# A two-layer encoder trunk: x of the first MLP through DRAM, and the last 16 adaLN vectors made in halves during that MLP's first product

## The chip, the cores and the metric

The kernel runs on one core of a Trainium2 chip. The metric is the device time of one execution in microseconds (us); lower is better. Below, PE is TensorE (matmuls), DVE is VectorE, ACT is ScalarE, POOL is GpSimd and SP is SyncE, whose queue issues nearly all DMAs here.

## The reference, cut to what matters

The input is one sequence of 1024 positions with 1024 channels, and one conditioning vector c. There are two layers. Each has a mixer and a channel MLP, and both are normed, shifted, scaled and gated by vectors that come from c:

```python
cond = silu(c)
for i in range(2):
    mod = cond @ ada_w[i] + ada_b[i]             # 6 vectors of 1024 for each layer
    sh1, sc1, g1, sh2, sc2, g2 = split(mod, 6)
    h = rmsnorm(x, norm1_g[i]) * (1 + sc1) + sh1
    y = gqa_attention(h) if i == 0 else chunked_gmlp(h)
    x = x + g1 * y
    h = rmsnorm(x, norm2_g[i]) * (1 + sc2) + sh2
    x = x + g2 * (square(relu(h @ w_in[i])) @ w_out[i])
```

The vectors sh1 to g2 are called j = 0 to 5 in the kernel. Each is kept as 8 columns of 128 values (k = 0 to 7), so "an adaLN vector" (layer, j, k) is here one column of 128 numbers: 128 dot products of length 1024.

## The kernel before, in words

Everything is held transposed: a tile has 128 channels on the partitions and 512 positions (one half, `hf`) along the free axis. x is 16 such tiles, `x[hf][m]`. They sit in the 16 slots of the tag "x" (`xslot()`), which attention used for its keys before, and which the gMLP uses for other things after writing x out.

Every product runs in fp32 by splitting each operand into a high and a low part and doing three matmuls (L415 to L417 in a first product, L1073 to L1075 in a second one). The splits are the steady work of ACT (high part, L287, L400, L1057) and DVE (low part, L288, L401, L1058). Large products use a seven-multiplication scheme on 2x2 blocks (q = "1" to "7"), with sums of weights and sums of activations made on DVE and POOL.

The stages in order of time are: attention; its output product (`wo_mm`, L792 to L796), which adds to x; the first MLP (`mlp(0, ...)`) with a first product (`winograd`, 112 units of 12 matmuls) and a second product (`Out`, 112 units); the gMLP with its v product, u product and `Out` product (84 units); and the second MLP, again two products.

In an MLP the first product's hook `at(i)` is called after unit i. At i = HB = 2 it starts the norm of the right half of x (`norm_ss`, `norm_rb`), and from then on `forms_b` reads `x[1]` through the next eight units. The left half was read earlier by `forms_a`. Then x rests until the second product adds to it (`Out.add`, L1089, `x = out * gate + x`). When a tile of x is finished, `done` squares it on ACT (L231) and adds the square up on POOL or DVE (L235) for the next norm.

The adaLN vectors are made in three ways. Some are made by `Slabs` on POOL during attention. Most are made by `mod_load`: a 512 KB DMA of 128 rows of the weight (L141), one DVE instruction over 128x1024 that multiplies by the broadcast silu(c) and sums along the row (L145), the read of its accumulator, and a small add of the bias (L148). 32 of the list `pending` are done this way by the end of the output product of attention. The last 16 (layer 1, j = 3 and 5) are left for later: 12 of them in the second product of the first MLP, at units 14, 17, ... 47 (`MO`), and 4 in the `Out` product of the gMLP at units 16, 20, 24, 28 (`MG`). For each of the two stages the broadcast c is loaded again (`load_cond`, L134) and passed through Silu on ACT (`silu_cond`, L137). Their buffers come from the pool "c", which `cut(4)` opens at unit 8.

The gMLP already sends x through DRAM: `spill(hf)` stores x to `xd` (L1279), the slots are used by the v and u products, and `load_xs` reads x back (L1525) around the start of its `Out` product.

The order of instructions on an engine's queue is made by a planner from operands, buffers and modelled times; an instruction wrapped in `pin(...)` stays behind all that was written before it on its engine. The `mod_load` DVE instruction and the Silu are pinned; DMAs of `spill` and `load_xs` are not. Once made, the order is fixed, and each engine works it off in order, waiting wherever an operand is late.

Of the kernel before, what the change touches and what calls it, by code (L numbers as in the profile page):

```python
# [11 lines left out]
F32 = mybir.dt.float32  # L12
F32R = mybir.dt.float32r
AF = mybir.ActivationFunctionType
ALU = mybir.AluOpType
# [3 lines left out]
P = 128  # L19
D = 1024  # L20
KT = 8
# [15 lines left out]
def encoder_kernel(ctx: ExitStack, tc: tile.TileContext, t: dict, out: bass.AP):  # L37
    nc = tc.nc
    V, S, G, T = nc.vector, nc.scalar, nc.gpsimd, nc.tensor

    const = ctx.enter_context(tc.tile_pool(name="const", bufs=1))
    small = ctx.enter_context(tc.tile_pool(name="small", bufs=3))
# [4 lines left out]
    def nm(s):  # L47
        uid[0] += 1
        return f"{s}_{uid[0]}"

    def pin(ins):
        tc.keep_in_program_order(ins)

    def slot(dt=F32, shape=(P, 512)):
        return mem.tile(list(shape), dt, tag="t", name=nm("t"), bufs=SLOTS["t"])

    def xslot(dt=F32):
        return mem.tile([P, 512], dt, tag="x", name=nm("x"), bufs=SLOTS["x"])


    part = {}

    def cut(n):
        if part:
            part["es"].close()
        es = ExitStack()
        part.update(es=es, n=n, pool=es.enter_context(tc.tile_pool(name=nm("part"), bufs=1)))

    def cwide(dt=F32, shape=(1024,)):
        return part["pool"].tile([P] + list(shape), dt, tag="c", name=nm("c"), bufs=4)  # L70
# [54 lines left out]
    mod = const.tile([P, 2, 6, KT], F32, name="mod")  # L125
    adab = const.tile([P, 2, 6, KT], F32, name="adab")
# [1 line left out]
    ng = const.tile([P, 2, 2, KT], F32, name="ng")  # L128
    amod = const.tile([P, 2, 2, KT], F32, name="amod")
    cond = []  # L130

    def load_cond(tile_):
        cond[:] = [tile_]
        nc.sync.dma_start(tile_, t["cond"].broadcast_to([P, D]))  # L134

    def silu_cond():
        pin(S.activation(cond[0], cond[0], AF.Silu))  # L137

    def mod_load(layer, j, k, tag="w", late=True):
        raw = wide(tag)  # L140
        ld = nc.sync.dma_start(raw, t["ada"][layer, j * KT + k])  # L141
        if tag == "w" and late:
            pin(ld)
        acc = mod[:, layer, j, k : k + 1]
        ins = V.scalar_tensor_tensor(raw, raw, 1.0, cond[0], ALU.mult, ALU.mult, accum_out=acc)  # L145
        if late:
            pin(ins)
        V.tensor_tensor(acc, acc, adab[:, layer, j, k : k + 1], ALU.add)  # L148

    def mod_scale(layer, which, k):  # L150
        V.scalar_tensor_tensor(amod[:, layer, which, k : k + 1], mod[:, layer, 3 * which + 1, k : k + 1],
                               1.0, ng[:, layer, which, k : k + 1], ALU.add, ALU.mult)

    pending = [(0, j, k) for j in (2, 4, 3, 5) for k in range(KT)]
# [48 lines left out]
    def mods(n, tag="w"):  # L203
        for _ in range(min(n, len(pending))):
            layer, j, k = pending.pop(0)
            mod_load(layer, j, k, tag)
            if j in (1, 4):
                mod_scale(layer, j // 3, k)
# [31 lines left out]
    def norm_ss(sqs, bank):  # L240
        acc = sqs.acc
        ps = bank("ss")[:, :4]
        for j in range(4):
            T.matmul(ps[:, j : j + 1], acc[:, j * P : (j + 1) * P], ones[:, 0:1], start=True, stop=True)
        ms = small.tile([P, 4], F32, tag="ms", name=nm("ms"))
        V.tensor_scalar(ms, ps, 1.0 / D, EPS, ALU.mult, ALU.add)
        r = rsqrt_small(ms, 4)
        dg = slot()
        for j in range(4):
            V.tensor_scalar_mul(dg[:, j * P : (j + 1) * P], ident, r[:, j : j + 1])  # L250
        return dg
# [59 lines left out]
    def more(f, n=1, left=0):  # L311

        while f["todo"] and (n > 0 or (left is not None and len(f["todo"]) > left)):
            f["todo"].pop(0)()
            n -= 1
# [433 lines left out]
    x = [[None] * KT, [None] * KT]  # L749
# [52 lines left out]
    with ExitStack() as es:  # L802
# [117 lines left out]
        for i in range(nu + 2):  # L920
# [7 lines left out]
            for op in ORDER.split():  # L928
                f, w, j = op[0], int(op[1]), int(op[2])
# [31 lines left out]
    dram = ctx.enter_context(tc.tile_pool(name="dram", bufs=1, space=bass.MemoryType.DRAM))  # L961
# [175 lines left out]
    def spread(tiles, dst, spare, eng):  # L1137

        b11, b12, b21, b22 = (tiles[a] for a in ((0, 0), (0, 1), (1, 0), (1, 1)))
        t3 = spare()  # L1140
        eng.tensor_tensor(t3, b22, b12, ALU.subtract)
        eng.tensor_tensor(b12, b12, b11, ALU.subtract)
        eng.tensor_tensor(b11, b22, b12, ALU.subtract)
        eng.tensor_tensor(b21, b21, b11, ALU.subtract)
        return [lambda: nc.sync.dma_start(dst["7"], t3), lambda: nc.sync.dma_start(dst["5"], b12),
                lambda: nc.sync.dma_start(dst["6"], b11), lambda: nc.sync.dma_start(dst["4"], b21)]

    def early(q):
        return {(0, 0): "1", (1, 0): "2", (1, 1): "3"}.get(q)

    def forms_dram(n):
        return [{q: dram.tile([P, 512], F32, name=nm("hf")) for q in OUT_FORMS} for _ in range(n)]

    def mlp(layer, f, sqB, done, hook):
        hidden = forms_dram(16)
        out_ = Out(t["wm"][layer], hidden, 4, mod[:, layer, 5])
        cut(8)
        quad = {}
        stores = []

        def sink(c, m, hf):
            S.activation(c, c, AF.Relu)
            S.activation(c, c, AF.Square)
            p = m // 2
            quad[(m, hf)] = c
            q = early((m % 2, hf))
            if q:
                nc.scalar.dma_start(hidden[p][q], c)
                if q == "1" and p < FIRST:
                    del quad[(m, hf)]  # L1170
                elif q == "2" and p < FIRST:
                    quad[(m - 1, 0)] = slot()
                    nc.sync.dma_start(quad[(m - 1, 0)], hidden[p]["1"])
            else:
                tiles = {(j, h): quad.pop((m + j, h)) for j in range(2) for h in range(2)}
                stores.extend(spread(tiles, hidden[p], slot, V))

        n = 16 * 7
        rest = []

        def at(i):
            more(f, RW, None)
            if i == HB:
                rest.append(norm_ss(sqB, bank_y))
            elif i == HB + 1:
                rest[:] = forms_b(f, x[1], layer, 1, norm_rb(rest[0], bank_y), "5473")
            elif i > HB and rest:
                rest.pop(0)()
            if stores and i % 7 > 0 and i % 7 != 6:
                stores.pop(0)()  # L1190
            out_.ahead(i - n)

        winograd(lambda m: t["wi"][layer, m], 16, f, sink, FIRST, at)
        while stores:
            stores.pop(0)()

        def at_out(i):
            if i == MO[0] - 6:
                cut(4)
                if pending:  # L1200
                    load_cond(cwide())
            elif pending and i == MO[0] - 2:
                silu_cond()
            if len(pending) > 4 and i >= MO[0] and (i - MO[0]) % MO[1] < MO[2]:
                mods(1, "c")
            if hook and i >= out_.n - out_.tail:
                hook(i - out_.n + out_.tail)

        out_.run(at_out, done)

    wo_sums(1)
# [34 lines left out]
    def norm_hook(layer, which, bank):  # L1246
# [11 lines left out]
        return hook  # L1258

    mlp(0, fA, sqB, add_sq, norm_hook(1, 0, bank_y))  # L1260


    pieces = {}
    for ct in range(24):
        i, r = divmod(ct, 3)
# [4 lines left out]
        else:  # L1270
            pieces[ct] = ((2 * i + 1, 0, P),)

    xd = [[dram.tile([P, 512], F32, name=nm("xd")) for _ in range(KT)] for _ in range(2)]
    vd = [[dram.tile([2, P, 2, 256], F32, name=nm("vd")) for _ in range(4)] for _ in range(6)]
    st = small.tile([P, 8, 6, 6], F32, tag="st", name="st", bufs=1)

    def spill(hf):
        for k in range(KT):
            nc.sync.dma_start(xd[hf][k], x[hf][k])  # L1279

    def wino_v(f, hook):

# [128 lines left out]
    def gmlp(f, sqB, done, hook):  # L1411
# [78 lines left out]
        for p in range(12):  # L1490
            i = 7 * p
# [27 lines left out]
        upto(n + 9)  # L1519
        while stores:  # L1520
            stores.pop(0)()
        def load_xs(hf, odd):
            for k in range(odd, KT, 2):
                x[hf][k] = xslot()
                nc.sync.dma_start(x[hf][k], xd[hf][k])  # L1525

        load_xs(0, 0)
        XL = {2: (0, 1), 6: (1, 0), 10: (1, 1)}

        def at_out(i):  # L1530
            if i == MG[0] - 6:
                cut(4)
                load_cond(cwide())
            elif pending and i == MG[0] - 2:
                silu_cond()
            if pending and i >= MG[0] and (i - MG[0]) % MG[1] < MG[2]:
                mods(1, "c")
            if i in XL:
                load_xs(*XL[i])
            if i >= out_.n - out_.tail:  # L1540
                hook(i - out_.n + out_.tail)
# [23 lines left out]
FA = 3  # L1565
LO = 3
TG = ((0, 0), (1, 0), (1, 1), (0, 1))
MO = (14, 3, 1)
MG = (16, 4, 1)
LW = 5  # L1570
IG = 30
SW = 3
# [4 lines left out]
HB = 2  # L1577
# [80 lines left out]
```

## Time and profile before

| | |
|---|---|
| median of 3 runs | 2747.19 us (2745.71 to 2747.94) |
| the profiled execution's own time | 2744.76 us |
| its span | 2742.9 us |
| first product of the first MLP | starts at 679.0 us |
| second product of the first MLP | starts at 1004.7 us |
| v product of the gMLP | starts at 1333.7 us |
| `Out` product of the gMLP | starts at 1857.3 us |
| first product of the second MLP | starts at 2109.9 us |
| second product of the second MLP | starts at 2426.3 us |

A table of windows gives, for a stretch "from:to" of the span, the stretch's length and then the busy time and the number of instructions (x) of PE, PEld (weight loads), DVE, ACT and POOL, then the granted TensorE clock, the DMA engines' busy share and the GB/s moved. A row of a source line gives the count, then minimum/median/maximum duration in ns, then when the first and the last one started, then the shapes. A row of waits reads: who waited, for whom, us in total, how many times, the longest. A row of the timeline has the start, the time taken, the instruction, and in brackets the idle time of the engine before it and what ended it.

### The profile page before, as it was taken

How to read it: one execution, taken by the hardware profiler on the slowest of the kernel's cores; microseconds unless marked ns; L12 is line 12 of the kernel's file. 1: busy time of each engine (PE TensorE's matmuls, PEld its weight loads, DVE VectorE, ACT ScalarE, POOL GpSimd, SP SyncE). 2: the span in 40 equal slices, each digit the busy share in tenths (PEclk: the TensorE clock that was granted, in tenths of full speed). 3: DMA queues.
4: the chain of work that ended last, by engine and by line, in shares of the span. 5: the costliest groups of instructions: out<-in, count | busy, mean ns of one | idle time of the engine just before them, and what ended most of it. 6: DMA issues, size and time to landing. Idle time of an engine off the chain costs nothing. (4 is left out here: it accounts for less than half of the span.)

```text
span 2742.9 us, 37309 instructions
## 1 busy us (share of the span) xinstructions
PE 2642.3 (96%) x12804; PEld 2184.9 (80%) x12804; DVE 2275.4 (83%) x3191; ACT 1454.5 (53%) x2598; POOL 1063.8 (39%) x716
## 2 busy tenths in 40 slices
PE   7889999999899999999999999999989999999999
PEld 5668999887688887777778888887868688878877
DVE  7889888888887778998797777787998887789993
ACT  4448999964644455435443355444436554554442
POOL 2448777534300024451543255556541400034520
PEclk9999999999999999999999999999999999999999
DMA  7241111225164458826244345558642364478462
GB/s 263 71 138 47 62 55 55 80 95 182 66 210 151 160 205 313 293 81 206 79 134 131 108 166 180 181 189 315 234 131 66 111 205 149 162 260 287 142 203 70
DMA packets 200544, 427.52 MB, mean 156 GB/s; under 512 B 23137, under 2 KB 35425, under 8 KB 200354
## 3 DMA queue, kind: packets, MB, share of 16 engines
q1 hardware_dynamic: 173474, 387.37, 41.6%
q10 hardware_dynamic: 26880, 37.76, 3.7%
q8 instruction: 101, 1.65, 0.2%
q14 instruction: 89, 0.73, 0.1%
HBM read 306.56 MB, written 118.49 MB: 155 GB/s over the span
## 5 line engine op out<-in xcount | busy, mean ns | idle before, releaser
L1074 PE MATMUL out<-t,s 128*128 128x512 f32 x1232 | 487.0, 396 | 14.3 <-DVE t L288 14.3
L1073 PE MATMUL out<-t,s 128*128 128x512 f32 x1232 | 487.0, 396 | 6.8 <-ACT t L287 6.8
L1075 PE MATMUL out<-t,s 128*128 128x512 f32 x1232 | 485.8, 395 | 6.0 <-DVE s L1058 5.7
L415 PE MATMUL w<-t,s 128*128 128x512 f32 x1168 | 460.1, 395 | 0.5 <-ACT t L287 0.5
L416 PE MATMUL w<-t,s 128*128 128x512 f32 x1168 | 455.5, 391 | 1.5 <-DVE t L288 1.1
L417 PE MATMUL w<-t,s 128*128 128x512 f32 x1168 | 454.9, 389 | 0.9 <-DVE s L401 0.9
L288 DVE TENSOR_TENSOR t<-t,t 128x512 fp32r<-128x512 f32 x408 | 377.9, 940 | 28.7 <-ACT t L287 21.2
L287 ACT CAST t<-t 128x512 fp32r<-128x512 f32 x408 | 244.3, 617 | 157.9 <-DMA t<-hf 65.2
L400 ACT CAST s<-w 128x512 fp32r<-128x512 f32 x292 | 174.3, 619 | 229.7 <-PE w L417 164.1
L1074 PEld LDWEIGHTS out<-t,s 128*128 128x128 f32 x1232 | 234.9, 191 | 70.7 <-DVE t L288 21.3
L1073 PEld LDWEIGHTS out<-t,s 128*128 128x128 f32 x1232 | 234.4, 190 | 60.1 <-ACT t L287 11.0
L1075 PEld LDWEIGHTS out<-t,s 128*128 128x128 f32 x1232 | 234.8, 191 | 59.3 <-DVE s L1058 11.1
L401 DVE TENSOR_TENSOR s<-w,s 128x512 fp32r<-128x512 f32 x292 | 227.9, 789 | 59.0 <-ACT s L400 55.4
L1044 POOL TENSOR_TENSOR w<-w,t 128x512 f32<-128x512 f32 x32 | 53.0, 1658 | 557.2 <-DMA t<-in_wm_dram 279.3
L416 PEld LDWEIGHTS w<-t,s 128*128 128x128 f32 x1168 | 219.4, 188 | 51.0 <-DVE t L288 6.7
L415 PEld LDWEIGHTS w<-t,s 128*128 128x128 f32 x1168 | 219.2, 188 | 49.6 <-issue 3.4
L417 PEld LDWEIGHTS w<-t,s 128*128 128x128 f32 x1168 | 219.3, 188 | 46.4 <-DVE s L401 1.3
L1058 DVE TENSOR_TENSOR s<-t,s 128x512 fp32r<-128x512 f32 x240 | 212.2, 886 | 49.2 <-ACT s L1057 46.4
L1057 ACT CAST s<-t 128x512 fp32r<-128x512 f32 x240 | 147.6, 620 | 188.7 <-PE out L1075 115.6
L860 DVE TENSOR_TENSOR t<-t,t 128x512 fp32r<-128x512 f32 x256 | 164.3, 683 | 20.9 <-ACT t L854 20.9
L837 DVE TENSOR_REDUCE mx<-s 128x1 f32<-128x1024 f32 x128 | 156.6, 1224 | 23.7 <-PE s L834 22.4
L870 PE MATMUL o<-t,t 128*128 128x256 f32 x1024 | 163.7, 293 | 0.0
(247 smaller groups left out, 5438.1 us busy)
## 6 DMA issues: line engine op xcount, KB each, us to landing
t<-hf SPq DMA_DIRECT2D x320, 256.0 KB, 4.5
hf<-c SPq DMA_DIRECT2D x156, 256.0 KB, 2.1
w<-in_wi_dram SPq DMA_DIRECT2D x64, 512.0 KB, 4.3
hf<-c ACTq DMA_DIRECT2D x96, 256.0 KB, 2.0
c<-in_ada_dram SPq DMA_DIRECT2D x36, 512.0 KB, 4.7
w<-in_adan_dram SPq DMA_DIRECT2D x32, 512.0 KB, 3.3
t<-in_wm_dram SPq DMA_DIRECT2D x64, 256.0 KB, 5.3
wf<-w SPq DMA_DIRECT2D x64, 256.0 KB, 3.3
```

What stands on the lines that cost most here:

```text
L287: S.copy(hi, src)
L288: (eng or V).tensor_tensor(lo, src, f32(hi), ALU.subtract)
L400: S.copy(hi, src)
L401: V.tensor_tensor(lo, src, f32(hi), ALU.subtract)
L415: T.matmul(ps, hi[:, a], th, start=kt == 0, stop=False)
L416: T.matmul(ps, hi[:, a], tl, start=False, stop=False)
L417: T.matmul(ps, lo[:, a], th, start=False, stop=kt == 3)
L860: pin(V.tensor_tensor(lo, pt, f32(hi), ALU.subtract))
L1058: V.tensor_tensor(lo, src, f32(hi), ALU.subtract)
L1073: T.matmul(ps, hi[:, a], th, start=begin and kt == 0, stop=False)
L1074: T.matmul(ps, hi[:, a], tl, start=False, stop=False)
L1075: T.matmul(ps, lo[:, a], th, start=False, stop=end and kt == 3)
```

## The change

`spill`, `load_xs` and the DRAM tiles `xd` move ahead of `mlp`, and the first MLP uses them too: at unit HB + 10 = 12 of its first product all of x is stored to DRAM, and x is read back around the start of its second product, in the same four groups as in the gMLP (before unit 0, and after units 2, 6 and 10). In between, the 16 x slots are free for the new class `Halves`. It loads c as two broadcast tiles of 128x512 and passes each through Silu. It then makes each of the 16 vectors that are left from two loads of 128x512 and two DVE instructions of that size, whose sums go to a small tile; after the eight vectors of one j, one small add joins the halves and one adds the bias, for all eight at once. As written, steps are taken at units 20, 25, ... 95 (MX = 5), two vectors are loaded ahead at unit 12, and one more at each step. None of the new instructions is pinned.

The second product of the first MLP and the `Out` product of the gMLP lose their loads of c, their Silu and their 12 and 4 vectors; only `cut(4)` stays at unit 8 (`CUT`).

```diff
-    def load_cond(tile_): ...
-    def silu_cond(): ...
+    xd = [[dram.tile([P, 512], F32, name=nm("xd")) for _ in range(KT)] for _ in range(2)]
+    def spill(hf):
+        for k in range(KT):
+            nc.sync.dma_start(xd[hf][k], x[hf][k])
+    def load_xs(hf, odd):
+        for k in range(odd, KT, 2):
+            x[hf][k] = xslot()
+            nc.sync.dma_start(x[hf][k], xd[hf][k])
+    XL = {-1: (0, 0), 2: (0, 1), 6: (1, 0), 10: (1, 1)}
+    class Halves:
+        def __init__(self, todo):
+            self.todo, self.raw, self.part = list(todo), [], {}
+        def start(self):
+            self.cond = [xslot(), xslot()]
+            for h in range(2):
+                nc.sync.dma_start(self.cond[h], t["cond"][:, h * 512 : (h + 1) * 512].broadcast_to([P, 512]))
+                S.activation(self.cond[h], self.cond[h], AF.Silu)
+        def load(self):
+            if self.todo:
+                layer, j, k = self.todo.pop(0)
+                raw = [xslot(), xslot()]
+                for h in range(2):
+                    nc.sync.dma_start(raw[h], t["ada"][layer, j * KT + k][:, h * 512 : (h + 1) * 512])
+                self.raw.append((layer, j, k, raw))
+        def step(self):
+            if not self.raw:
+                return
+            layer, j, k, raw = self.raw.pop(0)
+            self.load()
+            if k == 0:
+                self.part[j] = small.tile([P, 2, KT], F32, tag="half", name=nm("half"), bufs=2)
+            part = self.part[j]
+            for h in range(2):
+                V.scalar_tensor_tensor(raw[h], raw[h], 1.0, self.cond[h], ALU.mult, ALU.mult,
+                                       accum_out=part[:, h, k : k + 1])
+            if k == KT - 1:
+                V.tensor_tensor(part[:, 0], part[:, 0], part[:, 1], ALU.add)
+                V.tensor_tensor(mod[:, layer, j], part[:, 0], adab[:, layer, j], ALU.add)
 ...
+        halves = None if layer else Halves(pending)     # in mlp
         def at(i):
             more(f, RW, None)
+            if halves and i == HB + 10:
+                spill(0)
+                spill(1)
+                halves.start()
+                halves.load()
+                halves.load()
+            elif halves and i > HB + 16 and i % MX == 0:
+                halves.step()
 ...
         def at_out(i):                                  # second product of an MLP
-            if i == MO[0] - 6:
+            if i == CUT:
                 cut(4)
-                if pending:
-                    load_cond(cwide())
-            elif pending and i == MO[0] - 2:
-                silu_cond()
-            if len(pending) > 4 and i >= MO[0] and (i - MO[0]) % MO[1] < MO[2]:
-                mods(1, "c")
+            if halves and i in XL:
+                load_xs(*XL[i])
 ...
+        if halves:
+            load_xs(*XL[-1])
         out_.run(at_out, done)
 ...
         def at_out(i):                                  # Out product of the gMLP
-            if i == MG[0] - 6:
+            if i == CUT:
                 cut(4)
-                load_cond(cwide())
-            elif pending and i == MG[0] - 2:
-                silu_cond()
-            if pending and i >= MG[0] and (i - MG[0]) % MG[1] < MG[2]:
-                mods(1, "c")
 ...
-MO = (14, 3, 1)
-MG = (16, 4, 1)
+CUT = 8
+MX = 5
```

More of the change, by code (lines that the diff above doesn't have):

```diff
@@ L130, in encoder_kernel @@
     cond = []
[L132 to L137, printed above, removed]
     def mod_load(layer, j, k, tag="w", late=True):
@@ L1271, in encoder_kernel @@
             pieces[ct] = ((2 * i + 1, 0, P),)
-    xd = [[dram.tile([P, 512], F32, name=nm("xd")) for _ in range(KT)] for _ in range(2)]
     vd = [[dram.tile([2, P, 2, 256], F32, name=nm("vd")) for _ in range(4)] for _ in range(6)]
     st = small.tile([P, 8, 6, 6], F32, tag="st", name="st", bufs=1)
-    def spill(hf):
-        for k in range(KT):
-            nc.sync.dma_start(xd[hf][k], x[hf][k])
     def wino_v(f, hook):
@@ L1521, in gmlp @@
             stores.pop(0)()
[L1522 to L1528, printed above, removed]
+        load_xs(*XL[-1])
         def at_out(i):
-            if i == MG[0] - 6:
+            if i == CUT:
                 cut(4)
-                load_cond(cwide())
-            elif pending and i == MG[0] - 2:
-                silu_cond()
-            if pending and i >= MG[0] and (i - MG[0]) % MG[1] < MG[2]:
-                mods(1, "c")
             if i in XL:
```

## The prediction

> **What bounds the kernel now.** I read the page first, for the share of each engine.
>
> ```profile
> span 2742.9 us, 37309 instructions
> PE 2642.3 (96%) x12804; PEld 2184.9 (80%) x12804; DVE 2275.4 (83%) x3191; ACT 1454.5 (53%) x2598; POOL 1063.8 (39%) x716
> ```
>
> PE is the bound over the whole span, so an edit on another engine is worth only the PE waits that it takes away or makes. To find them I read windows of 50 us and counted matmuls.
>
> ```profile
> 640.00:690.00 50.00, 45.62 (x201) 36.56 (x199) 42.76 (x54) 28.96 (x45) 26.47 (x13) 0.99 0.43 145
> 690.00:740.00 50.00, 44.97 (x167) 34.70 (x168) 41.10 (x59) 29.33 (x52) 23.11 (x14) 0.87 0.15 53
> 740.00:790.00 50.00, 49.57 (x215) 39.66 (x214) 41.18 (x64) 22.73 (x41) 7.40 (x5) 1.00 0.52 179
> 840.00:890.00 50.00, 50.00 (x222) 41.42 (x221) 38.26 (x60) 24.71 (x43) 0.00 (x0) 1.00 0.42 150
> 940.00:990.00 50.00, 50.00 (x223) 41.40 (x222) 35.84 (x56) 25.29 (x43) 0.00 (x0) 1.00 0.41 148
> ...
> 1050.00:1100.00 50.00, 50.00 (x222) 41.42 (x221) 49.25 (x65) 24.63 (x44) 23.02 (x14) 1.00 0.84 301
> 1100.00:1150.00 50.00, 48.78 (x214) 39.41 (x213) 50.00 (x70) 21.28 (x37) 22.94 (x14) 1.00 0.80 268
> 1150.00:1200.00 50.00, 49.92 (x219) 40.37 (x217) 49.32 (x58) 15.80 (x28) 31.68 (x20) 1.00 0.41 141
> 1200.00:1250.00 50.00, 43.74 (x165) 33.32 (x165) 48.12 (x57) 21.26 (x39) 23.31 (x15) 0.90 0.43 138
> 1900.00:1950.00 50.00, 50.00 (x222) 41.44 (x221) 49.22 (x64) 26.69 (x46) 22.29 (x15) 1.00 0.91 330
> 1950.00:2000.00 50.00, 47.86 (x208) 38.60 (x207) 48.79 (x53) 17.73 (x31) 34.35 (x22) 1.00 0.48 168
> 2000.00:2050.00 50.00, 45.12 (x169) 35.26 (x169) 48.72 (x57) 21.28 (x39) 22.14 (x15) 0.86 0.43 133
> 2500.00:2550.00 50.00, 50.00 (x223) 41.39 (x222) 48.26 (x63) 24.56 (x44) 22.55 (x15) 1.00 0.73 238
> 2550.00:2600.00 50.00, 50.00 (x222) 41.42 (x221) 46.44 (x60) 20.50 (x36) 23.09 (x16) 1.00 0.50 167
> 2600.00:2650.00 50.00, 46.80 (x197) 37.58 (x197) 45.70 (x54) 18.07 (x34) 24.64 (x16) 0.97 0.50 162
> ```
>
> A stretch in which PE waits for nothing holds x222 or x223. So 50 / 222.5 = 0.225 us is lost for each matmul that is missing. The count also holds what a lowered clock costs (0.87 and 0.90 after long waits). Three kinds of stretch appear. In the first product from 840 us on PE is full and DVE has 12 to 14 us of 50 free. In the second product DVE is at 49 or 50 of 50. Around the turns of the stages (690 to 740, 1200 to 1250, 2000 to 2050) PE loses most.
>
> **What the vectors cost now.** Rows of their lines over 1000 to 2000 us:
>
> ```profile
> L145 DVE SCALAR_TENSOR_TENSOR c<-c,c x16: 1205/1211/2314, 1052.4 to 1946.6; 128x1024 f32<-128x1024 f32 x16
> L145 DVE DVE_READ_ACCUMULATOR c<-c,c x16: 72/78/84, 1053.6 to 1948.5; 128x1 f32 x16
> L148 DVE TENSOR_TENSOR mod<-mod,adab x16: 143/148/1254, 1054.2 to 1949.1; 128x1 f32<-128x1 f32 x16
> L1089 DVE SCALAR_TENSOR_TENSOR x<-out,mod,x x62: 735/740/752, 1022.2 to 1997.6; 128x512 f32<-128x512 f32 x62
> ```
>
> One vector takes 1.211 + 0.078 + 0.148 = 1.44 us of DVE. Twelve take 17.2 us out of the second product of the first MLP, between 1052 us and about 1150 us, and four take 5.7 us out of the gMLP's `Out` product.
>
> *Removed from the first MLP.* The waits of PE there, first from 1125 to 1190 us, then (three rows) from 1190 to 1255 us, and one wait of ACT from 1150 to 1260 us:
>
> ```profile
> PE out L1075 <- DVE s L1058: 1.2, 2, 0.8
> ...
> PE out L1074 <- DVE t L288: 4.0, 4, 1.7
> PE out L1073 <- ACT t L287: 1.5, 2, 1.1
> PE out L1075 <- DVE s L1058: 0.6, 1, 0.6
> ...
> ACT t L231 <- DVE x L1089: 24.3, 8, 7.9
> ```
>
> From 1100 to 1150 us 8.5 matmuls are missing (1.9 us), from 1150 to 1200 us 3.5 (0.8 us). The waits are for DVE's low part of the weights, at a DVE that is never idle. The same product of the second MLP carries no vectors; its stretches of the same place (2500 to 2600) hold x223 and x222, with DVE at 48.26 and 46.44. So these 2.7 us go. Next behind them is PE itself.
>
> *The tail behind it.* From 1200 to 1250 us 57.5 matmuls are missing: 12.9 us. There ACT stands in order at squares of finished x (L231), waiting for DVE's add, while a split stands behind. The gMLP's tail, 2000 to 2050, misses 53.5 (12.0 us) although its last vector starts at 1946.6, and there were only four. So the tail comes from the squares, adds and POOL sums at the turn, not from the vectors. I take 0 for it. The far bound is the second MLP's tail without squares, 25.5 missing (5.7 us): a gain of 12.9 - 5.7 = 7.2. I stay near 0 because the gMLP's row is the nearer one.
>
> *Removed from the gMLP.* PE is full while the four run (x222). From 1950 to 2000 us 14.5 are missing (3.3 us). Most of it belongs to the turn, so 0.5 of gain, bounds 0 and 3.3.
>
> **The halves, and where they land.** A half is the same operation over 128x512. The row of L1089 gives 0.74, and with the accumulator 0.82; two are 1.64, and 16 vectors 26.2 us, against 16 x 1.44 = 23.0 before. The first product's rows at 740, 840 and 940 leave DVE 8.8, 11.7 and 14.2 us free, 34.7 in these three stretches alone. What hides the halves is this idle DVE under a PE that is full, and POOL, which stretches DVE's work elsewhere (L145's 2.314 us), is at 0.00. Spread there they cost nothing. Without this cover they cost 26.2 us.
>
> But nothing pins them, and the trace shows what the planner does with unpinned work. The rows are the gMLP's own spill, SP's wait for it within 690 to 1310 us, the product in whose unit 2 it is written, and the start of the first MLP's first product:
>
> ```profile
> L1279 SPq DMA_DIRECT2D xd<-x x16: 319/320/320, 1198.7 to 1335.8; - x16
> SPq L1279 <- DVE x L1089: 82.7, 12, 26.1
> L1377 PE MATMUL v<-s,t x336: 388/389/1415, 1333.7 to 1575.4; 128*128 128x512 f32 x168
> ...
> L415 PE MATMUL w<-t,s x115: 387/389/496, 679.0 to 799.4; 128*128 128x512 f32 x115
> ```
>
> The stores begin 135 us before the product that they are written into, each right behind its last add. So the new spill will start in attention's output product, where x is finished, and not at unit 12. x[0] is read for the last time before the MLP's first matmul at 679.0 us, so its slots come free there; Silu and the first halves can follow at about 680 us. That is the densest place of this stage: 690 to 740 us holds x167, 55.5 missing (12.5 us). The rows there, DVE's and ACT's timeline, then the waits of PE from 676 to 760 us:
>
> ```profile
> 696.86 0.16 DVE L246 TENSOR_SCALAR ms<-ss 128x4 f32<-128x4 f32 x1 [3.82 <-PE ss L244]
> 702.51 2.50 DVE L293 TENSOR_TENSOR t<-x,t 128x512 f32<-128x512 f32 x4 [3.34 <-ACT t L257]
> 707.21 2.55 DVE L288 TENSOR_TENSOR t<-t,t 128x512 fp32r<-128x512 f32 x2 [0.86 <-ACT t L287]
> ...
> 695.36 0.59 ACT L420 COPY c<-w 128x512 f32<-128x512 f32 x1 [4.50 <-PE w L417]
> 697.05 0.21 ACT L213 ACTIVATE sd<-ms 128x4 f32<-128x4 f32 x1 [1.11 <-DVE ms L246]
> ...
> PE w L415 <- ACT t L287: 4.4, 3, 2.6
> PE w L417 <- DVE t L288: 4.1, 3, 1.6
> ```
>
> DVE idles three times on the chain of the norm of x[1]. A half put into such a gap can be late by up to its own 0.74, on average half: 3 x 0.37 = 1.1 us on PE, which waits for these splits. Bounds: 0 if no half stands there; the slow rival below if many do.
>
> *Silu.* Rows of its line and of the square root's table, over 640 to 2100 us:
>
> ```profile
> L137 ACT ACT_TABLE_LOAD x2: 1283/1283/1283, 1042.5 to 1900.4; - x2
> L137 ACT ACTIVATE c<-c x2: 1060/1062/1064, 1043.8 to 1901.7; 128x1024 f32<-128x1024 f32 x2
> L213 ACT ACT_TABLE_LOAD x4: 1283/1283/1283, 652.3 to 2054.3; - x4
> ```
>
> A switch of table takes 1.283 us. In the new place Silu (1.28 + about 1.1) fits into ACT's gap of 4.50; the switch back for the square root at 697.05 has a gap of 1.11, so 0.2 stays on the path. Bounds 0 and 2.5 (a switch and both Silus with no gap). What goes at 1042.5 and 1900.4 lies where PE does not wait for ACT: 0.
>
> The Trainium skill, "ScalarE: Activation LUTs", section "What ACT_TABLE_LOAD costs", says that a switch also drains, 2.66 us in all. By it the return would stay on the path with 1.5 us, and the sum below would be 1.4 worse. The trace does not bear this out: L137's load starts at 1042.5 and its ACTIVATE at 1043.8, with nothing between.
>
> *DMA and SP.* Added are 16 stores and 16 loads of 256 KB; the 16 vectors become 32 issues of the same bytes, and one load of c goes. The stores issue in 0.32 us each. SP waits in order behind them for x, as it does now (26.1 us at the longest). Behind them stand weight loads of the output product and of the MLP, which are prefetched by buffers that come free at the same pace. DMA engines are 0.43 busy from 640 to 690 us. I take 0, bounds 0 and 4 (one late weight tile, about the 4.4 us that PE waits for ACT's splits there). The loads of x are unpinned too and come with free slots well before the first add at 1022.2 us: 0.
>
> **Sum.** -2.7 - 0.5 + 1.1 + 0.2 = -1.9 us. Against the profiled execution's own 2744.76 us (span 2742.9 and 1.9 around it) that is 2742.9; it lies 2.4 below the median of the runs, 2747.19, so in their terms 2745.3.
>
> **Rivals.**
> *The tail shrinks too (faster).* The DVE that enters the tail is no longer behind, ACT's 24.3 us at L231 shorten, and the turn of 1200 to 1250 comes out as the second MLP's. For: DVE is at 49.32 up to 1200. Against: the gMLP's tail. -1.9 - 7.2 = -9.1: 2738.1.
> *The halves flood the start (slower).* One mechanism: the 16 slots less two for c hold seven vectors, and if the planner puts these 14 halves in before 740 us, each takes 0.74 of a DVE that PE waits for, or up to 1.78 where POOL's work holds it (POOL is at 23.11 of 50 there). Mean 1.26 x 14 = 17.6, less the idle 3.82 + 3.34 = 10.4; with the gains and Silu, -3.2 + 10.4 + 0.2 = +7.4: 2754.6. It decides from about nine halves in that stretch (9 x 1.26 - 7.2 = 4.1, more than the 3.0 gained). Against: DVE is at 41.10 with few real gaps, and these halves yield to all that is written before them. The Trainium skill, "SBUF — State Buffer", section on the shared port pair's exclusive lock, has DVE work with two SBUF inputs blocked for the whole of a POOL instruction; L145's maximum of 2.314 against 1.211 agrees.
> *The halves stay where they are written.* Then the start is untouched: -3.2, 2744.0.
>
> **How the numbers follow.** Forecast 0.43, halves as written 0.07, tail 0.26, flood 0.24. A change under 0.2% (5.5 us) can hardly be told from none. The first two are within it; tail gives faster 0.26, flood slower 0.24. The range reaches to both: 2738 to 2755; the likeliest's own, with its bounds, is 2741 to 2750.
>
> **What would show it.** Right: x222 from 1100 to 1200 us (in their shifted place) with DVE near 47; stores of x before 679 us; no 128x1024 DVE instruction of this kind after 1000 us; x222 from 840 to 990 us with DVE at 40 to 45; x160 to 167 from 690 to 740 us. Wrong: fewer than x150 from 690 to 740 us, a wait of PE on a late weight tile before 690 us, or a tail with under 45 missing.

## The result, and the profile after

The changed kernel is slower: 2752.29 us against 2746.26 us (medians of 17 runs each), a ratio of 1.0022 with a 95% interval of 1.0015 to 1.0029. The forecast was 2745.3, a gain of 1.9 us, which by its own account can hardly be told from no change. In pin_stt and in both runs of pin_loads_stt below, one execution came out far longer (3143 to 7478 us); their medians hold it, their ratios leave it out. Line numbers below are those of each kernel's own; the changed kernel's are 7 lower than before's up to the new code.

The page of the changed kernel, first lines:

```profile
span 2747.3 us, 37435 instructions
PE 2638.2 (96%) x12804; PEld 2184.7 (80%) x12804; DVE 2275.6 (83%) x3211; ACT 1452.0 (53%) x2597; POOL 1058.5 (39%) x716
```

DVE's sum is the same (2275.4 before). What moved is where its work stands. The windows of the same places, the second product's ones taken 14 us later and the gMLP's 7 us later for the shift up to there (the columns are those of the windows before):

```profile
640.00:690.00 50.00, 44.74 (x197) 35.81 (x195) 41.66 (x59) 27.31 (x40) 25.16 (x12) 1.00 0.64 210
690.00:740.00 50.00, 34.94 (x115) 24.64 (x115) 45.88 (x90) 23.26 (x38) 20.55 (x13) 0.76 0.78 252
740.00:790.00 50.00, 47.23 (x190) 35.84 (x191) 43.84 (x73) 27.44 (x49) 11.23 (x7) 0.97 0.53 172
840.00:890.00 50.00, 50.00 (x222) 41.40 (x222) 37.97 (x59) 24.64 (x42) 0.00 (x0) 1.00 0.43 149
...
1114.00:1164.00 50.00, 50.00 (x223) 41.40 (x222) 46.91 (x58) 20.95 (x39) 22.68 (x15) 1.00 0.70 228
1164.00:1214.00 50.00, 49.10 (x217) 40.37 (x216) 44.37 (x50) 16.10 (x29) 29.58 (x20) 1.00 0.24 78
1214.00:1264.00 50.00, 44.44 (x187) 34.84 (x185) 48.72 (x59) 21.89 (x40) 22.04 (x14) 0.97 0.45 153
...
1957.00:2007.00 50.00, 50.00 (x222) 41.44 (x221) 48.17 (x50) 18.41 (x32) 33.74 (x22) 1.00 0.44 152
```

Read the matmul counts. From 690 to 740 us x167 became x115 and from 740 to 790 us x215 became x190: 77 matmuls, 17 us, are lost at the start of the first MLP. DVE went from 41.10 to 45.88 there, and the granted clock from 0.87 to 0.76. Behind it counts rise: x214 to x223, and x165 to x187 in the tail; in the gMLP x208 to x222. Between the first two x219 became x217, because the shift shrinks there and the window reaches into the tail. Outside the tail DVE is no longer at 49 to 50 there, but at 44 to 48.

The positions of units, worked out from PE's own matmuls (12 to a unit), put this together. The first column is the start in the profile of before; the others say how much later (+) or earlier (-) the same unit starts, in us, in the changed kernel and in the main experiments below:

| first matmul of | before | changed | pin_spill | pin_stt | pinned halves | no vectors |
|---|---|---|---|---|---|---|
| first MLP, first product, unit 0 | 679.0 | +0.6 | +0.2 | +1.1 | -0.7 | -2.9 |
| unit 8 | 712.6 | +4.8 | -2.4 | +0.5 | -3.2 | -5.5 |
| unit 12 | 730.1 | +17.8 | -2.4 | +1.7 | -3.3 | -5.6 |
| unit 28 | 776.2 | +17.8 | +1.6 | +1.5 | -4.2 | -5.5 |
| unit 98 | 966.6 | +17.8 | +6.3 | +1.5 | -4.2 | -5.5 |
| second product, unit 14 | 1048.8 | +14.2 | +2.7 | -0.1 | -7.8 | -9.1 |
| unit 42 | 1125.0 | +14.2 | +2.7 | -0.1 | -7.8 | -8.0 |
| unit 68 | 1198.6 | +11.3 | -0.1 | -3.0 | -10.7 | -10.9 |
| unit 70 | 1208.8 | +7.8 | -3.7 | -7.8 | -14.1 | -14.2 |
| unit 84 | 1255.8 | +8.4 | -2.1 | -8.1 | -13.0 | -12.3 |
| gMLP, Out product, unit 42 | 1978.4 | +8.5 | -2.0 | -4.2 | -9.8 | -10.1 |
| unit 56 | 2023.3 | +2.2 | -6.9 | -10.0 | -16.7 | -16.9 |
| last matmul | 2738.8 | +4.4 | -5.7 | -7.4 | -17.1 | -15.6 |

So the change lost 17.2 us between units 0 and 28 of the first product and won about 13 back behind it. Of these 13, 3.6 come before unit 14 of the second product, ahead of the first vector.

Where all the halves went, and SP's row for the stores of x:

```profile
L1189 DVE SCALAR_TENSOR_TENSOR x<-x,x x32: 660/682/1778, 668.0 to 745.5; 128x512 f32<-128x512 f32 x32
L1189 DVE DVE_READ_ACCUMULATOR x<-x,x x32: 71/78/85, 668.7 to 747.2; 128x1 f32 x32
L1152 SPq DMA_DIRECT2D xd<-x x32: 319/323/642, 589.7 to 1343.7; - x32
```

All 32 halves stand between 668 and 747 us, though the program writes them at units 20 to 95 (about 757 to 961 us). The norm of the right half of x shows what that does. DVE's timeline there:

```profile
701.67 0.16 DVE L239 TENSOR_SCALAR ms<-ss 128x4 f32<-128x4 f32 x1 [1.42 <-PE ss L237]
701.75 0.68 DVE L1189 SCALAR_TENSOR_TENSOR x<-x,x 128x512 f32<-128x512 f32 x1
702.36 0.08 DVE L1189 DVE_READ_ACCUMULATOR x<-x,x 128x1 f32 x1
...
703.59 0.17 DVE L208 RECIPROCAL y<-sd 128x4 f32<-128x4 f32 x1
703.67 0.66 DVE L1189 SCALAR_TENSOR_TENSOR x<-x,x 128x512 f32<-128x512 f32 x1
704.26 0.08 DVE L1189 DVE_READ_ACCUMULATOR x<-x,x 128x1 f32 x1
704.26 0.16 DVE L210 TENSOR_TENSOR e<-y 128x4 f32<-128x4 f32 x1
704.34 0.68 DVE L1189 SCALAR_TENSOR_TENSOR x<-x,x 128x512 f32<-128x512 f32 x1
```

Between the small dependent steps of that norm (0.16 us each) the order has a half of 0.68, in front of nearly every one. From L239 (`ms`) to the first of the four L243 it takes 5.3 us (701.67 to 707.00), against 1.4 before (696.86 to 698.30).

The largest part of the loss comes behind the norm, though. By unit 8 the changed kernel is 4.8 us late, by unit 12 it is 17.8. Here are these four units, before and changed; the last row has DVE's busy time in the halves' instructions alone:

```profile
712.60:730.10 17.50, 13.52 (x49) 9.87 (x48) 17.09 (x19) 11.48 (x21) 12.64 (x9) 0.90 0.34 116
...
717.40:747.90 30.50, 20.56 (x48) 12.16 (x48) 29.87 (x42) 12.30 (x20) 18.68 (x12) 0.72 0.67 219
...
717.40:747.90 30.50, 12.56 (x22) 0.72 0.67 219
```

DVE was all but full in these units before (17.09 of 17.50 us). In the changed kernel 11 halves with their reads of the accumulator (x22) take 12.56 us of it, and the four units take 13.0 us longer. Two more things differ there: after the late norm, DVE starts on the right half of x 9.1 us later (711.64 us against 702.51), and the granted clock is lower (0.72 against 0.90). How much of the 13.0 each of the three makes was not separated.

And the waits of PE from 676 to 780 us, of which the largest before were 4.4 and 4.1 in total:

```profile
PE w L408 <- ACT t L280: 12.8, 4, 10.1
PE w L409 <- DVE t L281: 5.6, 5, 1.7
PE w L410 <- DVE t L281: 3.4, 3, 2.1
```

### The profile page after: what moved, and what is told of

Its sections match the earlier page's. It is cut to its first block, busy times and chain, and to the rows that moved or that the text cites. A ratio compares the mean times of both kernels' runs of the same rounds, so it can differ in the third digit from the quotient of the medians.

```text
span 2747.3 us, 37435 instructions
## 1 busy us (share of the span) xinstructions
PE 2638.2 (96%) x12804; PEld 2184.7 (80%) x12804; DVE 2275.6 (83%) x3211; ACT 1452.0 (53%) x2597; POOL 1058.5 (39%) x716
```

## The experiments

Every ratio is to the kernel before, which ran beside it. Two theories stood. **DVE:** the halves' instructions flood the start, where PE waits for DVE's splits. **SP:** the loads of halves and stores of x stand in SP's queue ahead of eight "passing" weight loads, which PE needs at once; they start at 690.1 us instead of 673.9, and SP waits 12.5 us (655 to 700 us) for slots that halves free. PE's wait of 10.1 us ends with ACT's cast of such a weight tile, which waited for its DMA:

```profile
L360 SPq DMA_DIRECT2D t<-in_wi_dram x16: 328/370/422, 690.1 to 2112.2; - x16
...
SPq L1177 <- DVE x L1189: 12.5, 9, 4.2
...
695.28 1.18 ACT L280 CAST t<-t 128x512 fp32r<-128x512 f32 x2 [3.29 <-DMA t<-in_wi_dram]
```

**Stores pinned (pin_spill).** The x slots can then not come free before unit 12.

```diff
-            nc.sync.dma_start(xd[hf][k], x[hf][k])
+            st_ = nc.sync.dma_start(xd[hf][k], x[hf][k])
+            if late: pin(st_)        # late in the first MLP only
```

> Only the 16 stores of x in the first MLP are pinned behind what SP has before unit 12; the halves stay free. Theory (the halves flood the start): slots of x then come free only after unit 12, so no half can stand before about 715 us; unit 28 of the first product comes at 776 to 780 us (before: 776.2, changed: 794.0), the gains behind stay (14 us by the profile), and the time is 2732 to 2738. Rival (sending x through DRAM and 8 MB of weights at this place costs the time by itself): unit 28 stays at 790 or later and the time at 2750 or more.

Measured: ratio 0.9972 (0.9963 to 0.9982), 2739.12 us. The halves stand from 741.3 to 846.3 us. Unit 28 is at +1.6 and the gains behind stay. x's way through DRAM is not the cause. But 4.7 us go between units 28 and 98, around three waits of 3.4 us in all (from 776 to 1004 us); before them DVE waited for MLP weights that were late (776 to 830 us):

```profile
PE w L410 <- DVE s L394: 3.4, 3, 1.4
...
DVE w L386 <- DMA w<-in_wi_dram: 5.0, 3, 1.9
```

**Passing loads on ACT's queue (passing_act).**

```diff
-                nc.sync.dma_start(passing[(q, p)], wsrc(2 * p)[:, i : i + 4])
+                nc.scalar.dma_start(passing[(q, p)], wsrc(2 * p)[:, i : i + 4])
```

> The changed kernel with the eight passing weight loads of the first product issued from ACT's queue instead of SP's. Theory SP (the wait of 10.1 us at 686 to 696 us comes from SP standing at loads of halves with the passing loads behind them): the passing loads go out near 674 us again, that wait falls under 3 us, unit 28 comes at about 786 and the time falls by 7 to 10 us to 2742 to 2745. Theory DVE (the 32 halves on DVE are what PE waits for): the wait moves to the next split and unit 28 stays within 3 us of 794; time 2749 to 2753.

Measured: 1.0007 (0.9997 to 1.0017), 2747.36 us; unit 28 at +14.6, which is 790.8 us. Time and unit lie in neither theory's range. It does not tell the theories apart, since the loads hardly moved: on ACT's queue they start at 689.1 us, right behind a square of x (L224) that waited 4.94 us for DVE and starts at the same time.

```profile
L360 ACTq DMA_DIRECT2D t<-in_wi_dram x16: 334/344/506, 689.1 to 2127.8; - x16
```

**Halves that cost DVE little (tiny_halves).** The loads and slots stay; each DVE instruction covers 8 of 512 columns.

```diff
-                V.scalar_tensor_tensor(raw[h], raw[h], 1.0, self.cond[h], ALU.mult, ALU.mult,
+                V.scalar_tensor_tensor(raw[h][:, :8], raw[h][:, :8], 1.0, self.cond[h][:, :8], ALU.mult, ALU.mult,
```

> The changed kernel with each half's DVE instruction over the first 8 columns only (the rest of each dot product is left out); the loads and their slots stay. Theory DVE: without some 30 us of DVE work in 668 to 747 us, unit 28 comes at 776 to 782 and the time is 2733 to 2740. Theory SP: the loads of halves still go out ahead of the passing loads, but their slots come free faster; unit 28 at 783 to 790 and the time 2741 to 2748.

Measured: 0.9974 (0.9965 to 0.9983), 2738.72 us; unit 28 at +3.5, so 14 of the 17 us are gone, though the passing loads still start at 687.8 us. That speaks for DVE, though the quick halves also free their slots sooner for SP (it waits 3.4 us for them instead of 12.5). Its window, x154 against x115:

```profile
690.00:740.00 50.00, 40.57 (x154) 30.75 (x155) 42.57 (x101) 28.48 (x49) 22.17 (x15) 0.88 0.79 272
```

**Only DVE's instructions pinned (pin_stt).** Loads and stores stay free.

```diff
-                V.scalar_tensor_tensor(raw[h], ..., accum_out=part[:, h, k : k + 1])
+                pin(V.scalar_tensor_tensor(raw[h], ..., accum_out=part[:, h, k : k + 1]))
```

> The changed kernel with only the DVE instruction of each half pinned (units 20 to 95); loads, Silu and the stores of x stay free. It leaves the queue's part of the loss and takes DVE's away. From the two runs before (a start loss of 17.8 us at unit 28; 14 of it gone with tiny halves, 3 with the passing loads on another queue) theory DVE: unit 28 at 776 to 781, time 2732 to 2737. Theory SP (loads of halves ahead of the passing loads): unit 28 at 785 or later, time 2741 or more.

Measured: 0.9971 (0.9958 to 0.9984), 2737.33 us; unit 28 at +1.5, inside theory DVE's 776 to 781. The passing loads start at 687.8 us here as well, and PE's first wait for them is still 5.5 us, but the waits after it are shorter, and units 0 to 28 lose 0.4 us in all:

```profile
PE w L408 <- ACT t L280: 7.2, 3, 5.5
PE w L410 <- DVE t L281: 3.4, 2, 2.9
PE w L409 <- DVE t L281: 0.7, 2, 0.5
```

So the early place of the halves makes the loss. This run does not fully part the two theories: with no half done before 760.8 us, SP does not wait for slots of theirs at the start either. In the changed kernel, what the late passing loads can have cost at once shows at unit 8 (4.8 us at most); units 8 to 12, where 13.0 us go, hold no wait for them. The norm starts late behind them and may carry some of it on; in pin_stt it starts 1.7 us late (4.8 in the changed kernel), and no such loss follows.

**x through DRAM alone (spill_only).** The kernel before with the stores and loads of x, and its vectors where they were.

```diff
+            if not layer and i == HB + 10:
+                spill(0)
+                spill(1)
...
+            if not layer and i in XL:
+                load_xs(*XL[i])
```

> The kernel before, its 16 vectors where they were, but x of the first MLP stored to DRAM and read back as in the changed kernel. Theory (the halves, not x's way through DRAM, make the loss): within 2 us of before, 2744 to 2748, unit 28 at 776 to 779. Rival (the stores on SP's queue hold up weight loads): unit 28 at 781 or later, 2750 or more.

Measured: 1.0009 (0.9999 to 1.0018), 2746.17 us; unit 28 at -0.9. The passing loads start at 687.9 us here too, behind stores and loads of x: nothing else takes the slots, so x comes back at once (661.4 to 717.8 us; in the changed kernel 722.2 to 747.7). So neither x's way through DRAM nor passing loads that are 14 us late cost anything that shows (the interval leaves room for 5 us). With the 13.0 us of units 8 to 12, theory SP falls as the main cause.

**No vectors at all (no_vectors).** The kernel before without the last 16.

```diff
-    pending += [(1, j, k) for j in (3, 5) for k in range(KT)]
+    V.memset(mod[:, 1, 3], 0.0)
+    V.memset(mod[:, 1, 5], 0.0)
 ...
```

> The kernel before without the last 16 vectors at all (they are set to 0), x kept in its slots. It gives what the vectors cost where they were. By the prediction's sum 3.2 us: 2743. If the changed kernel's profile is right (about 14 us gained behind the start): 2731 to 2734, with unit 70 of the first MLP's second product some 10 us and unit 56 of the gMLP's Out product some 4 to 6 us more ahead.

Measured: 0.9953 (0.9940 to 0.9967), 2732.31 us. Leaving the vectors out is worth 13 us by the runs, not 3.2. Unit 70 is 14.2 us earlier, where some 10 were expected. By the table only 6.5 us lie behind unit 14 of the second product, where the first vector stands (-9.1 to -15.6). 3.6 us lie in units 0 to 14, and 5.5 us ahead of that product. No vector stands in either place; why the first MLP starts 2.9 us earlier and gains another 2.6 in its first units was not found.

**Without the gMLP's four (no_gm4).** It tests the prediction's step that the tail does not come from the vectors.

```diff
-    pending += [(1, j, k) for j in (3, 5) for k in range(KT)]
+    pending += [(1, j, k) for j in (3, 5) for k in range(KT)][:12]
+    V.memset(mod[:, 1, 5, 4:], 0.0)
 ...
```

> The kernel before without the four vectors in the gMLP's Out product (the last four gate columns are set to 0); the first MLP's twelve stay. The prediction's step (the tail after the turn does not come from vectors that end 50 us ahead of it; 0.5 us): same stretch lost, 2745 to 2747. Theory backlog (DVE never idles between, so 5.7 us of its work is still owed at the turn): units 42 to 56 of that product 5 to 7 us shorter, the first MLP's unchanged, time 2739 to 2742.

Measured: 0.9989 (0.9980 to 0.9998), 2740.67 us. Units 42 to 56 of that product are 6.9 us shorter, as theory backlog has it; 3.7 us are lost earlier, in units 0 to 14, so the whole is worth less. How far DVE is behind there can be worked out: from the end of a unit's last matmul to the start of its add on DVE. At unit 40, 26 us after the last vector, it is 5.4 us in the kernel before and 0.0 in this one. Window of its stretch before the turn, and the same stretch of before:

```profile
1972.00:2022.00 50.00, 48.10 (x211) 39.16 (x211) 47.10 (x48) 19.32 (x34) 32.58 (x21) 1.00 0.35 108
...
1972.00:2022.00 50.00, 46.97 (x192) 37.54 (x191) 47.51 (x48) 17.79 (x32) 32.65 (x21) 0.93 0.31 97
```

**Halves pinned where they are written (pin_loads_stt), the best version.** Loads of the weight rows and DVE's instructions are pinned, and Silu.

```diff
-                    nc.sync.dma_start(raw[h], t["ada"][layer, j * KT + k][...])
+                    pin(nc.sync.dma_start(raw[h], t["ada"][layer, j * KT + k][...]))
...
-                V.scalar_tensor_tensor(raw[h], ...)
+                pin(V.scalar_tensor_tensor(raw[h], ...))
```

> The changed kernel with loads of halves, Silu and the DVE instructions pinned where they are written (units 12 to 95); the stores of x stay free. Theory (all of the loss is the place of the halves; spread over the full first product they cost nothing): unit 28 at 776 to 780, no more lost up to unit 98, the 12 to 14 us behind stay gained: 2731 to 2736, within 3 us of the kernel without the vectors (2732). Rival (26 us of DVE and 12 MB of DMA in that product cost PE something wherever they stand, as the 4.7 us between units 28 and 98 with pinned stores suggest): unit 98 at 971 or later, 2737 or more.

> The kernel of pin_loads_stt once more, for a profile at full clock and a closer time. Expected by theory flood, as before: 2730 to 2734 and a ratio of 0.995 to 0.997; unit 28 of the first product within 4 us of the kernel before; no loss between units 28 and 98; units 42 to 70 of the first MLP's second product 6 to 7 us shorter, units 42 to 56 of the gMLP's Out product 5 to 7. The rival (the product pays for the halves wherever they stand) has unit 98 at 971 or later.

Measured: 0.9958 (0.9945 to 0.9972), 2731.26 us, and 0.9962 (0.9948 to 0.9977), 2733.3 us. The second run's profile is the one read here and in the table. Halves, windows of the first product and of the turn:

```profile
L1189 DVE SCALAR_TENSOR_TENSOR x<-x,x x32: 681/689/1783, 755.7 to 958.4; 128x512 f32<-128x512 f32 x32
...
690.00:740.00 50.00, 45.58 (x183) 35.11 (x184) 42.79 (x63) 35.33 (x62) 18.00 (x11) 0.94 0.22 75
740.00:790.00 50.00, 49.98 (x221) 41.03 (x220) 48.93 (x81) 25.61 (x45) 12.49 (x8) 1.00 0.75 247
840.00:890.00 50.00, 50.00 (x222) 41.42 (x221) 41.43 (x76) 25.30 (x43) 0.00 (x0) 1.00 0.52 183
1092.00:1142.00 50.00, 50.00 (x222) 41.41 (x221) 47.08 (x59) 20.97 (x40) 22.86 (x15) 1.00 0.69 233
```

The halves stand from 755.7 to 958.4 us under a full PE (x222), with DVE at 41.43 instead of 38.26, and cost nothing that shows: units 28 and 98 have the same shift. Unit 28 is 4.2 us earlier than before, a little more than expected. The end is within 1.5 us of the kernel without vectors. The rival of that run falls.

## Why the prediction was wrong

**The halves' place: the step that failed most.** The prediction saw that the new stores would be planned far ahead (they start at 589.7 us, as it said) and that the first halves would follow near 680 us (668.0). It then priced them at three gaps with half a half each, 1.1 us. The runs showed 17.2: all 32 went in, most of the loss fell in units 8 to 12, where DVE had no gap left, and pin_stt, which pins only these instructions, takes the loss away. All three of the prediction's signs of being wrong came: x115 from 690 to 740 us, PE's wait for a late weight tile from 686 us on, and 35.5 missing in the tail's window.

The slow rival named the place and the mechanism but capped it at 14 halves, since the slots hold seven vectors. They hold seven at a time; each half that is done frees its slot for the next load, so there is no cap. That its 2754.6 lies 2.3 us from the measured time is luck: it added 10.4 for the halves where 17.2 were lost, and took off 3.2 where about 13 were gained. Its argument against, that the halves yield to all written ahead of them, did not hold on the chip: the order was fixed, and the norm's 0.16 us steps stood behind 0.68 us halves. The chance of 0.24 was too low for what the spill's rows already showed.

**The vectors' old cost: the step that failed next.** Predicted 2.7 + 0.5. The 2.7 of the stretch before the tail came out: units 42 to 68 (1125.0 to 1198.6 us) gained 2.9 in every kernel that took the twelve away. The zero for the tail did not: units 68 to 70 gained 2.9 to 4.7 more, though by unit 84 some of it was lost again (1.4 to 5.1 are left). Nor did the 0.5 of the gMLP: units 42 to 56 of its `Out` product gained 6.3 in the changed kernel and 6.9 without the four. The argument for zero was the gMLP's tail, which stood although its vectors ended 50 us ahead. no_gm4 shows that much of this tail was from those vectors too: DVE has no idle time in between, so the 5.7 us it was given were still owed at the turn. The row that was to show independence shared the cause. For the first MLP the same is argued from DVE's 50.00 and 49.32 of 50 us; no run took its twelve alone.

**A part with another reason.** Units 0 to 14 of the second product gained 3.6 us in the changed kernel, before any vector stood there. Silu, which stands there at 1042.5 us before, is not needed for it: no_gm4 keeps that Silu and gains 1.6. In these units a cast on ACT (L287) stands behind one that waits for POOL until 1030.48 us in the kernel before, and ahead of it in the kernel without vectors; the waits are the same, the order is not. pin_stt has 1.7 and spill_only 0.0 of it. It seems to come with the planned order; what in the planner turns it was not found.

**Right.** In the place of 1100 to 1150 us PE is full as forecast, x223 for x214; in that of 1150 to 1200 it is x217, not the x222 forecast, for the window reaches into the tail. In the first product PE is full from 840 us. x's way through DRAM and its DMAs cost nothing that shows (spill_only). The halves themselves: the row for the same size gave 0.82 us with the accumulator, measured 0.682 + 0.078 = 0.76. Silu's return switch stands at 701.49 us on the norm's chain, as said. Its own part was not tried alone, but in pin_stt it still stands there (698.06 us) and units 0 to 28 lose only 0.4.

```profile
L1170 ACT ACTIVATE x<-x x2: 627/630/633, 664.9 to 673.5; 128x512 f32<-128x512 f32 x2
L1170 ACT ACT_TABLE_LOAD x1: 1283/1283/1283, 663.3 to 663.3; - x1
```

**DVE in the first product.** Expected at 40 to 45 of 50 from 840 us on; measured 37.97, because the halves were over by then. With the halves pinned it is 41.43.

## What to carry to other kernels

When work is moved under an idle engine, check in the trace of before how early unpinned work of that kind is planned, and reckon with all of it going there, not only as much as there are buffers at once. Idle time of an engine is cover only in the place where the work will stand: the same 32 halves cost nothing that shows where DVE was busy for 38 of 50 us, and 13.0 us went in units 8 to 12 where it was busy for 17.09 of 17.50 and 11 of them stood. And where an engine is at 98% between two places, work given to it at the first is paid at the second: a wait far behind is no proof that it has another cause.

## What the runs showed that was not expected

Eight weight loads that came 14 us later (673.9 to 687.9 us) cost nothing in sum: PE's first wait grew from 2.6 to 4.9 us in spill_only and the later ones shrank, probably because DVE was the bound of that stretch either way (in the kernel before it is busy for all of 679 to 692 us). And 16 stores and 16 loads of x, with SP waiting in order for x, moved the whole by a ratio of 1.0009 (0.9999 to 1.0018).
